# Two layers on one core: row scales of two RMS norms moved behind the matrix products

## The chip, the cores and the metric

The kernel runs on one core of a Trainium2 chip. The metric is the device time of one execution in microseconds (us), median of the runs; lower is better. TensorE (PE, with its weight loads PEld) does the matrix products, VectorE (DVE), ScalarE (ACT) and GpSimd (POOL) the element work, and SyncE (SP) issues most DMA transfers. The engines run side by side and wait for each other on semaphores.

## The reference

Two blocks on 512 rows of width 1024, all in float32, one after the other. The change lies in the first block, in two of its norms and in what comes behind them:

```python
def rmsnorm(x, g):
    y = x * lax.rsqrt(jnp.mean(jnp.square(x), axis=-1, keepdims=True) + RMS_EPS)
    return y * g

def memory_cross_attention(h, mem_n, w_q, w_kv, w_o):          # 4 heads of 256, 256 memory rows
    q = (h @ w_q).reshape(B, S, XATTN_HEADS, XATTN_HEAD_DIM)
    k, v = jnp.split(mem_n @ w_kv, 2, axis=-1)                 # reshaped to heads
    s = jnp.einsum('bshd,bmhd->bhsm', q, k) * (XATTN_HEAD_DIM ** -0.5)
    prob = jax.nn.softmax(s, axis=-1)
    return jnp.einsum('bhsm,bmhd->bshd', prob, v).reshape(B, S, D_MODEL) @ w_o

def first_block(x, mem, ...):
    h = rmsnorm(x, norm_mix)
    p = h @ w_in
    y = jnp.concatenate([retention_mixer(p[..., :RET_PROJ], ...), rwkv7_mixer(p[..., RET_PROJ:], ...)], axis=-1)
    x = x + y @ w_out
    x = x + memory_cross_attention(rmsnorm(x, norm_xattn), rmsnorm(mem, norm_mem), xattn_w_q, xattn_w_kv, xattn_w_o)
    h = rmsnorm(x, norm_mlp)
    x = x + jnp.square(jax.nn.relu(h @ mlp_w_up)) @ mlp_w_down     # width 4096
    return rmsnorm(x, norm_final)
# second_block: gated attention and a gated spatial mix, then a last norm; the change does not touch it
```

## The kernel before

Every product is done in three passes: each operand is split into a rounded high part (h) and the rest (l), and high by high, high by low and low by high are summed in PSUM (`mm3` and the loops like it). The weights come as 189 units of 128x1024, 512 KB each, streamed by SP into three `raw` buffers; `pump` makes a high part with an ACT cast and a low part with a subtraction on POOL or DVE (POOL for all units of the stretch that changes), into four pairs of buffers.

The order of the PE instructions is written out by hand. `streams` runs one main generator and a queue of side generators; at each `yield` of the main one a step passes, and a side piece spawned with a delay of so many steps is written into the PE's order when its step comes. Behind a `yield` with a name a generator goes on when that flag is set. On the other engines and in SP's queue the order comes from a scheduler that runs when the program is built, and at run time every queue goes strictly in that order.

After the mixers (`mix`) the row blocks of 128 go through `x1` and `mlp`:

- `x1` adds `y @ w_out` in two column halves j of 512 with `quad`. For j = 0 the four row blocks share each unit and finish 6 matrix multiplications apart; for j = 1 (`outer`) all four units are there and each block b finishes on its own, 24 multiplications after the one before. `quad` yields in front of every fourth multiplication.
- `add_half` adds the half to x on DVE, squares it on ACT with a sum per row, and for j = 1 multiplies x by the norm's weight row on POOL into `xg` (line 957). The weight row is a 512 KB transfer, broadcast to all partitions (`gain`).
- `norm_end` (lines 966 to 976) sums the squares, takes the root on DVE (`norm_scale`, `rsqrt`: eleven small instructions in a chain, lines 353 to 362 and 962, 963), scales `xg` by it (line 972), and 8 steps later `transp` turns the block on PE, eight 128x128 pieces into two PSUM tiles "tp" (of which there are two), each split by one ACT copy (872) and one DVE subtraction (873) of 128x512. Then the flag `norm b` is set.
- `tile_half` then multiplies the turned rows, three units for columns (rows of x) 0 to 255, then for 256 to 511: 72 multiplications of 256 columns each. Its second half waits for `norm 3`.
- The heads of the cross attention follow, with `softmax` on 128x256 tiles, then `x1`'s second pair of quads (`xattn_w_o`) with the same norm steps for `norm_mlp`, a second `tile_half` and the feed forward (`mlp`), whose sums go to x with `add_x`.

Of the kernel before, what the change touches and what calls it, by code (L numbers as in the profile page):

```python
# [82 lines left out]
def pack(inputs):  # L83

    f = {k: np.asarray(v) for k, v in inputs.items()}
# [19 lines left out]
    r, k, v = (wr[:, i * 512:(i + 1) * 512] for i in range(3))  # L105
# [71 lines left out]
    for name, key in (("w0", "rwkv_w0"), ("a0", "rwkv_a0"), ("k_k", "rwkv_k_k"), ("k_a", "rwkv_k_a"), ("r_k", "rwkv_r_k"),  # L177
# [5 lines left out]
    rows = np.concatenate([f[n].reshape(-1) for n in (  # L183
        "norm_mix", "norm_mem", "norm_xattn", "norm_mlp", "norm_final", "norm_gain_2", "final_gain_2",
        "ln_v_gain_2", "ln_v_bias_2", "q_gain_2", "k_gain_2", "b_spatial_2")])[None]
    c, cs = constants()
# [4 lines left out]
        "pos": np.ascontiguousarray(f["positions"].reshape(NB, P).T),  # L191
        "wst": np.ascontiguousarray(np.stack(units)),
        "pv": pv,
        "rows": np.ascontiguousarray(rows),
        "cst": c,
        "cs2": cs,
# [32 lines left out]
class Kern:  # L229
# [712 lines left out]
    def add_half(self, st, b, j, ps, scale=None):  # L942

        nc = self.nc
        self.add_x(b, j, ps, scale)
        x = self.x[b]
        if j == 0:
            st[b] = [self.small(3, "ss"), None]
            nc.scalar.activation(self.tmp(), x[:, 0:512], AF.Square, accum_out=st[b][0][:, 0:1])
            return  # L950
        self.flags.discard(f"norm {b}")
        ss, st[b][1] = st[b][0], self.tmp((P, 1024), "t4", 2)
        for i in range(4):
            c = slice(i * 256, i * 256 + 256)
            if i > 1:
                nc.scalar.activation(self.tmp((P, 256)), x[:, c], AF.Square, accum_out=ss[:, i - 1:i])
            nc.gpsimd.tensor_tensor(st[b][1][:, c], x[:, c], st["g"][:, c], op=ALU.mult)

    def norm_scale(self, ss, scale=1.0 / D, eps=1e-6):
        V = self.nc.vector  # L960
        v = self.small(1)
        V.tensor_reduce(v, ss, axis=AX.X, op=ALU.add)
        V.tensor_scalar(v, v, scale, eps, op0=ALU.mult, op1=ALU.add)
        return self.rsqrt(v, 1)

    def norm_end(self, st, b, dst, rs=None, wait=None):

        ss, xg = st[b]
        rs = self.norm_scale(ss) if rs is None else rs
        for h in range(2):  # L970
            c = slice(h * 512, h * 512 + 512)
            self.nc.vector.tensor_scalar(xg[:, c], xg[:, c], rs, None, op0=ALU.mult)
        yield 8
        self.transp(xg, b, dst)
        self.flags.add(f"norm {b}")

    def x1(self):
        st = {"g": self.gain("norm_xattn", 4)}
        hh, hx = self.act4((7, 8, 5, 9))

        def main():
            y1 = self.y1
            yield from self.quad(lambda k: y1[k], lambda b, ps: self.add_half(st, b, 0, ps))
            yield from self.quad(lambda k: y1[k], lambda b, ps: self.x1_post(st, b, ps, hh), outer=True)
            q = {}

            def put(t, ps):
                h = t // 2
                if t % 2 == 0:
                    q[h] = self.slab(12 + h % 2, [P, 2, 2, 512], F32R)  # L990
                self.psplit((q[h][:, 0, t % 2], q[h][:, 1, t % 2]), ps)
                if t % 2:
                    self.spawn(self.head(h, q[h]), 2)

            self.O = {}
            yield "norm 1"
            for t, ps in enumerate((yield from self.tile_half(hx, ("mm",) * 3, "norm 3"))):
                put(t, ps)
            for t in range(3, 8):
                put(t, (yield from self.tile_t(hx)))  # L1000
            st2 = self.st2 = {"g": self.gain("norm_mlp", 13)}
            self.hm, self.hmt = self.act4((2, 3, 0, 1))
            o = lambda k: self.O[k // 2][k % 2]
            yield from self.quad(o, lambda b, ps: self.add_half(st2, b, 0, ps), [f"head {h}" for h in range(4)])
            yield from self.quad(o, lambda b, ps: self.x1_post(st2, b, ps, self.hm), outer=True)

        return main()

    def rest(self):
        yield from self.x1()  # L1010
        yield from self.mlp()

    def x1_post(self, st, b, ps, dst):
        self.add_half(st, b, 1, ps)
        self.spawn(self.norm_end(st, b, dst))

    def head(self, h, q):

        pt = self.slab(4 if h % 2 == 0 else 6, [P, 2, 2, 512], F32R)

        def score(b):
            c = slice(b * 128, b * 128 + 128)
            sc = self.psum("tp", (P, 256))
            for k in range(2):
                self.mm3(sc, (q[:, 0, k, c], q[:, 1, k, c]), (self.mk[0][:, 2 * h + k], self.mk[1][:, 2 * h + k]), k == 0, k == 1)
            p = self.softmax(sc, 256, 1.0 / 16)
            yield 3
            tr = self.psum("ch", (P, 2, 128))
            for m in range(2):
                self.T.transpose(tr[:, m], p[:, m * 128:m * 128 + 128], self.ident)  # L1030
            self.psplit((pt[:, 0, :, c], pt[:, 1, :, c]), tr)

        for b in range(NB):
            self.spawn(score(b))
            yield 2
        yield 3 + 2
        o = self.slab((10, 11, 7, 8)[h], [P, 2, 2, 512], F32R)
        for d in range(2):
            ps = self.psum("ch")
            c = slice(h * 256 + d * 128, h * 256 + d * 128 + 128)  # L1040
            for m in range(2):
                self.mm3(ps, (self.mv[0][:, m, c], self.mv[1][:, m, c]), (pt[:, 0, m], pt[:, 1, m]), m == 0, m == 1)
            self.psplit((o[:, 0, d], o[:, 1, d]), ps)
            yield 1
        yield 1
        self.O[h] = [(o[:, 0, d], o[:, 1, d]) for d in range(2)]
        self.flags.add(f"head {h}")

    def softmax(self, sc, n, scale):

        nc = self.nc
        m, s = self.small(1), self.small(1)
        nc.vector.tensor_reduce(m, sc, axis=AX.X, op=ALU.max)
        nc.vector.tensor_scalar(m, m, -scale, None, op0=ALU.mult)
        p = self.tmp((P, n))
        nc.scalar.activation(p, sc, AF.Exp, bias=m, scale=scale, accum_out=s)  # L1056
        nc.vector.reciprocal(s, s)
        nc.vector.tensor_scalar(p, p, s, None, op0=ALU.mult)
        return p


    def mlp(self):
        nc = self.nc
        free = [4, 5, 6, 9, 10, 11, 7, 8]
        us = {}
        cur = {}

        def up(t, ps):
            if t % 2 == 0:
                cur["s"] = self.slab(free[(t // 2) % len(free)], [P, 2, 2, 512], F32R)  # L1070
            o = cur["s"]
            r, q = self.tmp(), self.tmp()
            nc.scalar.activation(r, ps, AF.Relu)  # L1073
            nc.gpsimd.tensor_tensor(q, r, r, op=ALU.mult)  # L1074
            self.split((o[:, t % 2, 0], o[:, t % 2, 1]), q)
            us[t] = (o[:, t % 2, 0], o[:, t % 2, 1])

        def main():
# [7 lines left out]
            for g in range(3):  # L1086
                for j in range(2):
                    for i in range(4 * j, 4 * j + 4):
                        up(8 * (g + 1) + i, (yield from self.tile_t(self.hmt)))
                    yield from self.quad(lambda k: us[8 * g + k], lambda b, ps: self.add_x(b, j, ps))  # L1090
            self.h2, self.h2t = self.act4((2, 3, 0, 1))

            def post(b, j, ps):

                self.add_x(b, j, ps)
                if j == 0:
                    self.flags.discard(f"norm {b}")
                    s0[b], s1[b] = self.small(4, "ss"), self.small(4, "ss")
                for i in (2 * j, 2 * j + 1):
                    x = self.x[b][:, i * 256:i * 256 + 256]  # L1100
                    nc.scalar.activation(self.tmp((P, 256)), x, AF.Square, accum_out=s0[b][:, i:i + 1])
                    nc.gpsimd.tensor_tensor(x, x, g1[:, i * 256:i * 256 + 256], op=ALU.mult)
                    nc.scalar.activation(self.tmp((P, 256)), x, AF.Square, accum_out=s1[b][:, i:i + 1])
                if j:
                    self.spawn(fin(b))
# [20 lines left out]
            for j in range(2):  # L1126
                yield from self.quad(lambda k: us[24 + k], lambda b, ps: post(b, j, ps), outer=True)
            yield from self.second()

        return main()  # L1130


# [570 lines left out]
```

## Time and profile before

| | us |
|---|---|
| median of 3 runs | 1331.93 |
| lowest and highest run | 1331.39, 1334.37 |
| the profiled execution, its own time | 1330.39 |
| its span, first to last instruction | 1328.6 |

All rows below come from the profiled execution. Its mean granted TensorE clock is 0.976 of full speed. The page gives busy times over the span; the chain of waits is followed back from the last instruction; the timeline lists instructions in order of time and, in square brackets, how long the engine stood idle before one and what ended that; the windows give busy time by stretch. PE is busy for 95% of the span, so what counts is where PE stands still or runs at a lower clock, and what it waits for there.

### The profile page before, as it was taken

To read this page: it belongs to the slowest core of one execution; us is meant where nothing else is said; L and a number is where in the kernel's file an instruction comes from. 1 tells how busy PE (TensorE), PEld (TensorE's weight loads), DVE (VectorE), ACT (ScalarE), POOL (GpSimd) and SP (SyncE) were. 2 spreads that over 40 slices of the span, in tenths; PEclk is the share of its full clock that TensorE was granted. 3 is DMA by queue.
4 is the path that set the end of the run, shared out by engine and by line. 5 is a ranking of instruction groups with operands and counts; after the bars stand their busy time and mean duration, and the time that the engine had idled before them with its cause. 6 is when DMAs were issued, how large, how long until landed. Compare 5 with 4: busy or idle time off the path is not lost.

```text
span 1328.6 us, 18213 instructions
## 1 busy us (share of the span) xinstructions
PE 1257.8 (95%) x6988; PEld 1043.1 (79%) x6988; DVE 699.8 (53%) x1465; ACT 507.7 (38%) x899; POOL 536.7 (40%) x544
## 2 busy tenths in 40 slices
PE   4999799998997989998999999999999999999997
PEld 4667577887895888888888888888887888788886
DVE  5667424456495275546333333332779946665355
ACT  5434323333344234433433322332534435554332
POOL 4924545135666553246311111110214563222474
PEclk9989899899999999999999999999999999999999
DMA  5223313211234422313333233333332232122321
GB/s 188 76 62 83 76 53 72 74 56 41 80 113 143 141 64 80 95 49 111 111 95 96 95 95 96 96 100 100 101 114 80 80 111 64 48 64 64 111 80 64
DMA packets 52376, 117.06 MB, mean 88 GB/s; under 512 B 23072, under 2 KB 23712, under 8 KB 52288
## 3 DMA queue, kind: packets, MB, share of 16 engines
q1 hardware_dynamic: 52112, 115.82, 28.6%
q8 instruction: 55, 0.90, 0.3%
q14 instruction: 33, 0.27, 0.1%
q0 software_dynamic: 32, 0.00, 0.0%
q10 hardware_dynamic: 144, 0.07, 0.0%
HBM read 112.46 MB, written 3.41 MB: 87 GB/s over the span
## 4 chain that ended last, share of the span: by engine, by line
PE 78%; POOL 7%; DVE 7%; issue 3%; ACT 2%; DMA 2%; SPq 0%; DVEq 0%; ACTq 0%; POOLq 0%
PE mm L220 64%; PE ch L220 7%; PE tp L220 4%; POOL s L220 3%; PE cs L220 3%; POOL o L1581 1%; DVE sm L362 1%; POOL s L1583 1%; DVE s L873 1%; DVE sm L358 1%; DMA s<-x 1%; DMA s<-dm 1%; POOL wl L220 0%; ACT t L1056 0%; ACT wh L291 0%
## 5 line engine op out<-in xcount | busy, mean ns | idle before, releaser
L220 PE MATMUL mm<-s,wh 128*128 128x512 f32 (+1 forms) x1424 | 422.5, 378 | 0.0
L220 PE MATMUL mm<-wh,s 128*128 128x512 f32 (+1 forms) x1264 | 364.1, 364 | 7.8 <-DVE s L873 7.8
L220 PEld LDWEIGHTS mm<-s,wh 128*128 128x128 f32 x1424 | 259.1, 191 | 53.2 <-issue 9.7
L220 PEld LDWEIGHTS mm<-wh,s 128*128 128x128 f32 x1264 | 231.2, 192 | 47.2 <-DVE s L873 9.6
L220 PE MATMUL mm<-s,wl 128*128 128x512 f32 (+1 forms) x704 | 263.5, 374 | 0.0
L291 ACT CAST wh<-raw 128x1024 fp32r<-128x1024 f32 x151 | 158.6, 1051 | 250.2 <-PE mm L220 220.2
L292 POOL TENSOR_TENSOR wl<-raw,wh 128x1024 fp32r<-128x1024 f32 x75 | 180.5, 2408 | 156.7 <-ACT wh L291 140.5
L220 PE MATMUL mm<-wl,s 128*128 128x512 f32 (+1 forms) x632 | 227.0, 359 | 2.0 <-POOL wl L292 1.7
L292 DVE TENSOR_TENSOR wl<-raw,wh 128x1024 fp32r<-128x1024 f32 x76 | 95.3, 1253 | 120.9 <-ACT wh L291 120.6
L220 PEld LDWEIGHTS mm<-s,wl 128*128 128x128 f32 x704 | 134.2, 191 | 21.3
L220 PEld LDWEIGHTS mm<-wl,s 128*128 128x128 f32 x632 | 121.9, 193 | 19.1 <-POOL wl L292 2.1
L1074 POOL TENSOR_TENSOR t<-t 128x512 f32<-128x512 f32 x32 | 50.0, 1563 | 214.8 <-ACT t L1073 214.8
L220 PE MATMUL mm<-s,whx 128*128 128x512 f32 (+1 forms) x336 | 100.2, 378 | 0.0
L220 PE MATMUL mm<-whx,s 128*128 128x512 f32 (+1 forms) x272 | 86.5, 377 | 0.6 <-DVE s L873 0.6
L347 DVE TENSOR_TENSOR s<-t,s 128x512 fp32r<-128x512 f32 x44 | 38.6, 877 | 69.9 <-ACT s L346 69.9
L292 POOL TENSOR_TENSOR wlx<-raw,whx 128x1024 fp32r<-128x1024 f32 x18 | 43.7, 2426 | 75.0 <-ACT whx L291 75.0
L220 PEld LDWEIGHTS mm<-s,whx 128*128 128x128 f32 x336 | 62.2, 194 | 10.6 <-DVE s L873 0.4
L220 PE MATMUL ch<-s,s 128*64 128x64 f32 (+3 forms) x504 | 65.2, 274 | 2.5 <-DVE s L873 1.8
L938 DVE TENSOR_TENSOR s<-mm,s 128x256 f32<-128x256 f32 x96 | 35.7, 419 | 58.7 <-PE mm L220 58.5
L291 ACT CAST whx<-raw 128x1024 fp32r<-128x1024 f32 x35 | 36.8, 1052 | 70.6 <-PE mm L220 54.4
L220 PE MATMUL mm<-s,wlx 128*128 128x512 f32 (+1 forms) x168 | 63.2, 376 | 0.0
L220 PEld LDWEIGHTS ch<-s,s 128*64 128x64 f32 (+2 forms) x504 | 47.0, 154 | 16.5 <-DVE s L873 3.7
(268 smaller groups left out, 1703.6 us busy)
## 6 DMA issues: line engine op xcount, KB each, us to landing
raw<-wst SPq DMA_DIRECT2D x189, 512.0 KB, 3.6
s<-x SPq DMA_DIRECT2D x8, 512.0 KB, 5.6
s<-rows SPq DMA_DIRECT2D x7, 512.0 KB, 4.0
out<-t SPq DMA_DIRECT2D x8, 256.0 KB, 2.3
t<-mem SPq DMA_DIRECT2D x2, 512.0 KB, 3.9
dm<-s SPq DMA_DIRECT2D x10, 64.0 KB, 2.0
s<-dm SPq DMA_DIRECT2D x2, 256.0 KB, 4.3
s<-dm SPq DMA_DIRECT2D x8, 64.0 KB, 2.5
```

Source lines behind the costliest of these rows:

```text
L220: r = getattr(self.eng, name)(*a, **k)
L291: (SC or nc.scalar).copy(h, r)
L292: (E or (nc.gpsimd if self.lowpart(self.nspl) else nc.vector)).tensor_tensor(l, r, h.bitcast(F32), op=ALU.subtract)
L347: self.nc.vector.tensor_tensor(dst[1], src, dst[0].bitcast(F32), op=ALU.subtract)
L358: V.scalar_tensor_tensor(t, y, h, y, op0=ALU.mult, op1=ALU.mult)
L362: V.scalar_tensor_tensor(y, t, 1.5, y, op0=ALU.add, op1=ALU.mult)
L873: (V or self.nc.vector).tensor_tensor(dst[1], ps, dst[0].bitcast(F32), op=ALU.subtract)
L938: self.nc.vector.tensor_tensor(xs, ps[:, c], xs, op=ALU.add)
L1074: nc.gpsimd.tensor_tensor(q, r, r, op=ALU.mult)
L1581: G.tensor_tensor(tv, w[:, 0:k, s:s + 1].broadcast_to([P, k, n]), m[:, s:s + 1, s + 1:32].broadcast_to([P, k, n]), op=ALU.mult)
L1583: G.tensor_tensor(w[:, 0:k, s + 1:32], w[:, 0:k, s + 1:32], tv, op=ALU.add)
```

## The change

The rows are turned without their scale, and without the weight. The weights of the two norms come as 16 columns in one small transfer (`gcol`, 64 bytes per partition) and are applied per partition in the split behind the turn: for each 128x128 piece one ACT copy with a scale and one DVE `scalar_tensor_tensor`, in place of one copy and one subtraction for four pieces. Each half is turned as soon as it is summed: half 0 of block b 3 + b steps after its sum, half 1 three steps after. One chain of roots over all four blocks (four columns) replaces the four chains. For the cross attention the scale goes into the softmax (as the scale of the exponential, and negated for the maximum); behind the squared ReLU of the feed forward the square of the scale is applied where the sums are added to x, so that 64 additions become `scalar_tensor_tensor`. The POOL multiplications by the weight rows and the two 512 KB transfers are gone.

```diff
+    def turn_half(self, st, b, j, ps, dst, delay):
+        nc = self.nc
+        self.add_x(b, j, ps)
+        if b + j == 0:
+            st["ss"] = self.small(8, "ss")
+        x = self.x[b][:, j * 512:j * 512 + 512]
+        if j:
+            self.flags.discard(f"norm {b}")
+
+        def turn():
+            h, l = dst[j]
+            c = slice(b * 128, b * 128 + 128)
+            tr = self.psum("tp", (P, 4, 128))
+            for k in range(4):
+                self.T.transpose(tr[:, k], x[:, k * 128:k * 128 + 128], self.ident)
+            for k in range(4):
+                g = st["g"][:, 4 * j + k:4 * j + k + 1]
+                nc.scalar.activation(h[:, k, c], tr[:, k], AF.Copy, scale=g)
+                nc.vector.scalar_tensor_tensor(l[:, k, c], tr[:, k], g, h[:, k, c].bitcast(F32), op0=ALU.mult, op1=ALU.subtract)
+            nc.scalar.activation(self.tmp(), x, AF.Square, accum_out=st["ss"][:, 2 * b + j:2 * b + j + 1])
+            if j == 0:
+                return
+            self.flags.add(f"norm {b}")
+            if b == NB - 1:
+                yield 5
+                v = self.small(4)
+                nc.vector.tensor_reduce(v, st["ss"].rearrange("p (b j) -> p b j", j=2), axis=AX.X, op=ALU.add)
+                nc.vector.tensor_scalar(v, v, 1.0 / D, 1e-6, op0=ALU.mult, op1=ALU.add)
+                st["scale"](self.rsqrt(v, 4))
+
+        self.spawn(turn(), delay)
+
     def x1(self):
-        st = {"g": self.gain("norm_xattn", 4)}
+        rows = self.mp.tile([P, 28], F32, name="rows")
+        g, self.sq, self.sm2 = rows[:, 0:16], rows[:, 16:24], rows[:, 24:28]
+        self.nc.sync.dma_start(g, self.A["gcol"])
+        def scale_q(rs):
+            V.tensor_scalar(self.sq[:, 0:4], rs, 1.0 / 16, None, op0=ALU.mult)
+            V.tensor_scalar(self.sq[:, 4:8], rs, -1.0 / 16, None, op0=ALU.mult)
+            self.flags.add("scale")
+        def scale_m(rs):
+            V.tensor_tensor(self.sm2, rs, rs, op=ALU.mult)
...
-            yield from self.quad(lambda k: y1[k], lambda b, ps: self.add_half(st, b, 0, ps))
-            yield from self.quad(lambda k: y1[k], lambda b, ps: self.x1_post(st, b, ps, hh), outer=True)
+            yield from self.quad(lambda k: y1[k], lambda b, ps: self.turn_half(st, b, 0, ps, hh, 3 + b))
+            yield from self.quad(lambda k: y1[k], lambda b, ps: self.turn_half(st, b, 1, ps, hh, 3), outer=True)
...
     def head(self, h, q):
+        yield "scale"
...
-            p = self.softmax(sc, 256, 1.0 / 16)
+            p = self.softmax(sc, 256, self.sq[:, b:b + 1], self.sq[:, b + 4:b + 5])
...
-                    yield from self.quad(lambda k: us[8 * g + k], lambda b, ps: self.add_x(b, j, ps))
+                    yield from self.quad(lambda k: us[8 * g + k], lambda b, ps: self.add_x(b, j, ps, self.sm2[:, b:b + 1]))
```

`norm_end` and `x1_post` are removed; the pair of quads before the feed forward changes in the same way, with the second eight weight columns and `scale_m`.

## Rows read from the trace of the kernel before

**Rows 1.** The page: busy time, share of the span, instructions of PE.
```profile
PE 1257.8 (95%) x6988; PEld 1043.1 (79%) x6988; DVE 699.8 (53%) x1465; ACT 507.7 (38%) x899; POOL 536.7 (40%) x544
```

**Rows 2.** PE timeline at both norms: start, us, engine, what, count, idle before.
```profile
476.78 0.51 PE L220 MATMUL mm<-s,whx 128*128 128x256 f32 x2
...
482.31 1.06 PE L220 MATMUL tp<-ident,t 128*128 128x128 f32 x8 [4.20 <-DVE t L972]
...
601.20 0.56 PE L220 MATMUL mm<-s,whx 128*128 128x256 f32 x2
...
606.78 1.94 PE L220 MATMUL tp<-ident,t 128*128 128x128 f32 x8 [4.20 <-DVE t L972]
```

**Rows 3.** Chain of waits in order of time, 480 to 500 us: start, us, what.
```profile
483.37 7.24 PE mm L220 x48
490.61 0.87 PE tp L220 x8
491.49 8.63 PE mm L220 x72
```

**Rows 4.** The same chain at the second norm, 600 to 616 us.
```profile
608.72 6.20 PE mm L220 x48
...
615.79 9.23 PE mm L220 x77
```

**Rows 5.** Timeline of DVE and POOL, 473 us: a root's step beside a split.
```profile
473.13 2.41 POOL L292 TENSOR_TENSOR wlx<-raw,whx 128x1024 fp32r<-128x1024 f32 x1 [0.55 <-ACT whx L291]
473.19 2.37 DVE L362 SCALAR_TENSOR_TENSOR sm<-sm,sm 128x1 f32<-128x1 f32 x1
```

**Rows 6.** Windows: stretch, length, busy of PE, PEld, DVE, ACT, POOL; clock, DMA.
```profile
482.30:486.30 4.00, 3.99 (x23) 4.00 (x24) 3.12 (x10) 2.81 (x7) 2.81 (x3) 0.63 0.52 135
...
606.70:609.20 2.50, 2.42 (x12) 2.45 (x13) 1.67 (x8) 1.75 (x5) 1.41 (x2) 0.50 0.80 198
...
340.00:350.00 10.00, 10.00 (x64) 7.36 (x64) 3.35 (x7) 2.14 (x4) 6.68 (x11) 1.00 0.30 97
```

**Rows 7.** Groups by line and form, ACT: count, busy us, mean ns, idle before.
```profile
L784 ACT ACTIVATE t<-tp,pv 128x128 f32<-128x128 f32 x16 | 6.0, 459 | 0.0
L872 ACT CAST s<-mm 128x128 fp32r<-128x128 f32 x4 | 1.1, 272 | 0.0
L949 ACT ACTIVATE t<-s 128x512 f32<-128x512 f32 x12 | 7.6, 630 | 7.0 <-DVE s L938 4.7 <-DVE s L940 2.3
```

**Rows 8.** The same for DVE.
```profile
L873 DVE TENSOR_TENSOR s<-mm,s 128x128 fp32r<-128x128 f32 x4 | 1.1, 287 | 0.5 <-ACT s L872 0.4
L938 DVE TENSOR_TENSOR s<-mm,s 128x256 f32<-128x256 f32 x96 | 35.7, 419 | 58.7 <-PE mm L220 58.5
L940 DVE SCALAR_TENSOR_TENSOR s<-mm,s 128x256 f32<-128x256 f32 x16 | 6.0, 420 | 19.0 <-PE mm L220 19.0
```

**Rows 9.** Timeline of ACT and DVE, 1013 us: two splits of one PSUM tile.
```profile
1013.35 0.58 ACT L1204 CAST s<-tp 64x512 fp32r<-64x512 f32 x1 [0.87 <-DVE s L1205]
1012.63 0.68 DVE L1205 TENSOR_TENSOR s<-tp,s 64x512 fp32r<-64x512 f32 x1
1013.97 0.69 DVE L1205 TENSOR_TENSOR s<-tp,s 64x512 fp32r<-64x512 f32 x1 [0.65 <-ACT s L1204]
```

**Rows 10.** Timeline of DVE and ACT, end of the second pair's first quad.
```profile
573.78 0.76 DVE L938 TENSOR_TENSOR s<-mm,s 128x256 f32<-128x256 f32 x2 [5.49 <-PE mm L220]
575.14 0.76 DVE L938 TENSOR_TENSOR s<-mm,s 128x256 f32<-128x256 f32 x2 [0.60 <-PE mm L220]
577.91 1.04 ACT L291 CAST wh<-raw 128x1024 fp32r<-128x1024 f32 x1
```

**Rows 11.** Waits of SP's queue for the weight rows' transfers, 325 to 400 us.
```profile
SPq L376 <- PE cs L220: 9.0, 1, 9.0
```

**Rows 12.** Timeline of SP and DVE, 405 to 415 us, end of the mixers.
```profile
405.34 0.33 SPq L281 DMA_DIRECT2D raw<-wst  x1
413.27 1.67 DVE L785 SCALAR_TENSOR_TENSOR t<-t,kt 128x512 f32<-128x512 f32 x1 [1.14 <-ACT t L784]
```

More of the change, by code (lines that the diff above doesn't have):

```diff
@@ L193, in pack @@
         "pv": pv,
+        "gcol": np.ascontiguousarray(np.concatenate([f[n].reshape(8, P).T for n in ("norm_xattn", "norm_mlp")], 1)),
         "rows": np.ascontiguousarray(rows),
@@ L950, in add_half @@
             return
-        self.flags.discard(f"norm {b}")
         ss, st[b][1] = st[b][0], self.tmp((P, 1024), "t4", 2)
@@ L964, in norm_scale @@
         return self.rsqrt(v, 1)
[L966 to L975, printed above, removed]
-    def x1(self):
-        st = {"g": self.gain("norm_xattn", 4)}
+    def x1(self):
+        rows = self.mp.tile([P, 28], F32, name="rows")
+        g, self.sq, self.sm2 = rows[:, 0:16], rows[:, 16:24], rows[:, 24:28]
+        self.nc.sync.dma_start(g, self.A["gcol"])
+        V = self.nc.vector
+        def scale_q(rs):
[4 more added lines that the diff above has]
+            V.tensor_tensor(self.sm2, rs, rs, op=ALU.mult)
+        st = {"g": g[:, 0:8], "scale": scale_q}
         hh, hx = self.act4((7, 8, 5, 9))
@@ L1000, in main @@
                 put(t, (yield from self.tile_t(hx)))
-            st2 = self.st2 = {"g": self.gain("norm_mlp", 13)}
+            st2 = {"g": g[:, 8:16], "scale": scale_m}
             self.hm, self.hmt = self.act4((2, 3, 0, 1))
             o = lambda k: self.O[k // 2][k % 2]
-            yield from self.quad(o, lambda b, ps: self.add_half(st2, b, 0, ps), [f"head {h}" for h in range(4)])
-            yield from self.quad(o, lambda b, ps: self.x1_post(st2, b, ps, self.hm), outer=True)
+            yield from self.quad(o, lambda b, ps: self.turn_half(st2, b, 0, ps, self.hm, 3 + b), [f"head {h}" for h in range(4)])
+            yield from self.quad(o, lambda b, ps: self.turn_half(st2, b, 1, ps, self.hm, 3), outer=True)
         return main()
@@ L1011, in rest @@
         yield from self.mlp()
-    def x1_post(self, st, b, ps, dst):
-        self.add_half(st, b, 1, ps)
-        self.spawn(self.norm_end(st, b, dst))
     def head(self, h, q):
+        yield "scale"
         pt = self.slab(4 if h % 2 == 0 else 6, [P, 2, 2, 512], F32R)
@@ L1047, in head, with softmax @@
         self.flags.add(f"head {h}")
-    def softmax(self, sc, n, scale):
+    def softmax(self, sc, n, scale, minus=None):
         nc = self.nc
@@ L1053, in softmax @@
         nc.vector.tensor_reduce(m, sc, axis=AX.X, op=ALU.max)
-        nc.vector.tensor_scalar(m, m, -scale, None, op0=ALU.mult)
+        nc.vector.tensor_scalar(m, m, -scale if minus is None else minus, None, op0=ALU.mult)
         p = self.tmp((P, n))
@@ L1089, in main @@
                         up(8 * (g + 1) + i, (yield from self.tile_t(self.hmt)))
-                    yield from self.quad(lambda k: us[8 * g + k], lambda b, ps: self.add_x(b, j, ps))
+                    yield from self.quad(lambda k: us[8 * g + k], lambda b, ps: self.add_x(b, j, ps, self.sm2[:, b:b + 1]))
             self.h2, self.h2t = self.act4((2, 3, 0, 1))
             def post(b, j, ps):
-                self.add_x(b, j, ps)
+                self.add_x(b, j, ps, self.sm2[:, b:b + 1])
                 if j == 0:
```

## Prediction, made before the change was run

> **What bounds the kernel now.** I read the page first: PE is busy for 95% of the span [rows 1], so time can be won only where PE stands still or runs slowly. Next comes PE's timeline with its idle times at the two norms that change. At each of them PE begins the 256-column products of `tile_half`, stops after nine, and stands for 4.20 us until DVE's line 972 has scaled a block [rows 2]. The third view says why line 972 is late: a step of the root, on one number per partition, takes 2.37 us on DVE while POOL runs a 2.41 us weight split [rows 5]; the chain of roots holds several of these, and DVE's queue behind it holds the last block's additions. The windows show what the stop leaves behind: the granted clock of the four microseconds after the first stop is 0.63 of full speed, and 0.50 in the 2.5 us after the second [rows 6]. Of the two levels that is the 1.2 GHz one for a good part of these stretches; PE had stood still before.
>
> **What the two stops cost.** From the first product of `tile_half` to the end of the second group of eight turns, the first norm takes 491.49 - 476.78 = 14.71 us and the second 615.79 - 601.20 = 14.59 us [rows 2 to 4]. In each lie 9 + 48 = 57 products and two groups of eight turns. Undisturbed, 72 such products take 8.63 us, so 0.120 each, and a group of turns 0.87 us [rows 3]. That makes 57 x 0.120 + 2 x 0.87 = 8.57 us. The stops with their slow clock cost 6.14 and 6.02 us, together 12.2 us. This is what the change can win; PE's own work (products, number of turns) stays as it is.
>
> **Part 1: turning without the scale.** The last block's turn now waits only for its addition to x. It is due three steps behind its sum, which comes out as nine 256-column products into `tile_half`: 9 x 0.120 = 1.08 us after the last sum. The addition ends about 0.03 + 0.76 = 0.8 us after it [rows 10], so PE waits 0 here, 0.3 us at most. The splits of that turn must be ready for the second half of `tile_half`, 72 products (8.6 us) after its start; they need about 1.1 + 0.4 + 3.7 = 5.2 us (part 2). `norm 1`, for the first half, is set two blocks earlier. Both stops go: -12.2 us. Next late behind them would be the weights: their splits in this stretch no longer wait behind POOL's multiplications, and one 2.4 us split [rows 5] per unit of 24 products (5.4 us) leaves room.
>
> **Part 2: the split in four pieces.** Per half block there are four ACT copies and four DVE operations of 128x128, where one of 128x512 each stood. How long is one of them? For ACT the nearest rows are 0.27 us (a plain 128x128 cast from PSUM) and 0.46 us (128x128 with two per-partition operands) [rows 7]; I take 0.40, as there is one such operand. For DVE they are 0.29 us (128x128 from PSUM) and 0.42 us (256 columns with a per-partition scale) [rows 8]; I take 0.31. Do the two engines overlap on one PSUM tile? In the second block two ACT copies and two DVE subtractions of different halves of one tile do not: the second copy stands until the first subtraction ends (1012.63 + 0.68 = 1013.31, start 1013.35), and the second subtraction starts 0.04 us after the copy [rows 9]. So four pieces alternate: 4 x (0.40 + 0.04 + 0.31 + 0.04) = 3.2 us, bounds 2.6 and 3.8. The square (0.63 us [rows 7]) overlaps only the last DVE piece, so a half block takes about 3.7 us, 3.1 to 4.3.
>
> The Trainium skill, PSUM — Partial Sum Buffer, section "PSUM bank collisions raise a hardware error", gives the reason: two engines must not touch one bank in the same quadrant of partitions in the same cycle, reads included, and the compiler's scheduler orders them. It speaks against this change, and the trace agrees (0.04 us handovers). Had the pieces overlapped, a half block would take 4 x 0.40 + 0.31 = 1.9 us and the wait below would be nil.
>
> PE feels this through the two "tp" tiles: the turn after next waits until the split has freed one. Count from the first block's sum, with 1.36 us per six products [rows 10], so 0.227 each, and 0.44 us per half turn (half of 0.87). By the order written out, turns of half 0 come behind 10, 18, 30 and 38 products, at 2.3, 4.5, 7.7 and 9.9 us; those of half 1 behind 50 and 74, at 13.1 and 19.0, and the others are wider apart. With 3.7 us the splits end at 6.4, 10.1, 13.8 and 17.5. The fourth turn waits 0.2 us for the second split, the fifth 0.5 for the third, the sixth not at all. At 3.1 us nothing waits; at 4.3 the two wait 1.4 and 1.1, 2.5 us. I take 0.7 us per norm, 1.4 in all, 0 to 5. A weight cast may stand behind the first turn's copies in ACT's queue: the fourth unit's, which starts at 577.91 when PE has freed its buffer [rows 10], 4.2 us in this count. Behind a split that ends at 6.4 it takes 1.04, and its low part 2.41 on POOL: 9.9 us, where PE needs it at about 9.7 (37 products and three half turns). So 0.2 us, 1.3 if an addition comes between; it is in the same 0 to 5.
>
> **Part 3: one chain for the roots.** Fourteen small instructions, and two for the scales, come once instead of four chains of eleven. They begin behind the last square, some 7 us after the sums, and the first exponential that needs them comes after the whole of `tile_half`, at least 17 us after. Even with three stalls of 2.4 us [rows 5] in about 3 us of work, they end 13 us after the sums. Cost nothing; if that cover were gone, PE would stand for a few us behind the first head.
>
> **Part 4: additions with a scale.** The 64 additions of the feed forward change from a plain addition to the form that the kernel's last norm already uses: 420 ns against 419 [rows 8]. Nothing.
>
> **Part 5: transfers and POOL.** Two 512 KB transfers go. Before one of them SP stood 9.0 us with the weight transfers behind it [rows 11], yet PE was busy for all of 340 to 350 us [rows 6]: no gain. The POOL multiplications are gone; POOL's work beside them was not late for PE except through DVE. The small transfer takes their place in SP's queue: nothing, if it doesn't stand there (rival 2).
>
> **Sum.** -12.2 + 1.4 = -10.8 us. The profiled execution took 1330.39 us (its span of 1328.6 and 1.8 around it) and would take 1319.6; the median of the runs is 1.54 us above that execution, so I predict 1331.93 - 10.8 = 1321.1 us.
>
> **Rivals.** (1) The alternation costs more: foreign work (casts, additions) stands in most splits, the "tp" waits come to 2.5 us per norm and the fourth unit is late by 1 us; the gain is 12.2 - 7 = 5 us: 1327. For it speaks that both engines carry casts and additions in these stretches; against it, that the turns of half 1 are 5.4 us and more apart, so that a backlog from half 0 drains.
>
> (2) Slower: the small transfer stands at the head of SP's queue. Its tile lies in memory that the mixers used. If that is a tile which the last retention block still reads (DVE's line 785, until 413.27 + 1.67 = 414.94 us [rows 12]), and it is queued ahead of the weight transfer of 405.34, that and those behind it are 9.6 us late, in a stretch where each unit feeds only 12 products (2.7 us). The gain of 10.8 us then shrinks to about 1 us: 1331. Each weight transfer further up that it is queued ahead of adds that one's distance; from 11 us of standing on the kernel is slower, and at 15 us it takes 1336. For it: the large transfers that it replaces did stand at the head of the queue [rows 11]. Against it: the tile is tiny and the first of its pool, so that it probably lies over something that was done with early.
>
> (3) The gain goes back to a resource behind the norms: the heads or the feed forward find a weight late, since PE arrives 6 us earlier. Same time, 1331. Against it: between the norms PE works without a wait, and a unit lasts 5.4 us there, over twice its split on POOL.
>
> (4) Orders shift and DVE meets fewer POOL splits at the end of the mixers, too: 3 us more gain, 1317.
>
> (5) The shared port: rows 5 show a DVE step with two inputs in SBUF standing for a POOL instruction. The pieces' DVE operations read PSUM and SBUF. If they stood as well, for 1.2 us (half a split) once in a half block, it would take 4.9 us, and the fourth and fifth turn would wait 2.6 and 1.7: 4.3 us per norm, gain 12.2 - 8.6 = 3.6 us, 1328. Against it: 96 additions of that form average 419 ns in stretches full of POOL work [rows 8]. [...]
>
> **Chances.** Forecast 0.62 (1318 to 1324), rival 1 0.14, rival 2 0.06, rival 3 0.07, rival 4 0.07, rival 5 0.04. From the median a difference below 0.2% (2.7 us) is about what a measurement of this kernel can't tell from no change. Faster takes the forecast, rivals 1, 4 and 5, less a little of rival 1: 0.85. Same: rival 3 and the mild form of rival 2, 0.08. Slower: the hard form of rival 2 and shifts of order that I can't see, 0.07. The range goes from rival 4, 1316, to 1329, past rivals 1 and 5; rivals 2 and 3 are left out.
>
> **What would show it.** In the profile after: no idle time of 4 us in PE before the turns, and a clock of 1.00 through both `tile_half` stretches; two stretches of some 8.6 + 0.4 us where 14.7 and 14.6 stood (there with two groups of turns); ACT and DVE alternating on "tp" with 0.04 us between; PE idle before half turns by some tenths, released by DVE; 420 ns for line 940 in the feed forward. The prediction is wrong if PE waits for the weight splits in the second quads, for "tp" tiles by over 2 us per norm, or if SP stands for the small transfer with weights behind it.

## The result, and the profile after

The changed kernel takes 1323.47 us, median of 8 runs (1318.68 to 1329.04), where the kernel before, run beside it, takes 1331.66 (8 runs, 1327.70 to 1334.37): a ratio of 0.9941, 95% interval 0.9917 to 0.9966. The same kernel once more, in the first experiment below, gave 0.9953 (0.9932 to 0.9974). One execution in each of norm1_only, norm2_only and norm1_64 ran at a much lower clock and is left out of their ratios; the one of norm1_64 is the profiled one (1407.51 us), so that run has no row in the table of leads. The profiled execution took 1326.15 us with a span of 1324.1, against 1330.39 and 1328.6 before. In this kernel the line numbers are higher: 221 is PE's helper, 292 and 293 are the weight casts and splits, 978 and 979 the two pieces of a turned block, 987, 988 and 354 to 363 the chain of roots.

Both stops are gone. This is PE's timeline at both norms (start, us, engine, what, count, and in brackets the idle time before it and what ended it), beside [rows 2]; the second and the fourth lines are the last half turn behind nine products of `tile_half`, where PE stood for 4.20 us before:

```profile
458.00 0.66 PE L221 MATMUL tp<-ident,s 128*128 128x128 f32 x4 [0.54 <-DVE s L979]
...
480.73 0.60 PE L221 MATMUL tp<-ident,s 128*128 128x128 f32 x4
...
577.75 0.66 PE L221 MATMUL tp<-ident,s 128*128 128x128 f32 x4 [0.48 <-DVE s L979]
...
600.42 0.60 PE L221 MATMUL tp<-ident,s 128*128 128x128 f32 x4
```

Windows from the start of each `tile_half` to 9 us behind it (length, busy time of PE, PEld, DVE, ACT, POOL, granted clock, DMA) answer [rows 6]: PE has no gap, and the clock is at its upper level throughout, where 0.63 and 0.50 stood.

```profile
479.60:488.60 9.00, 9.00 (x77) 8.96 (x75) 7.92 (x23) 3.62 (x9) 6.39 (x3) 1.00 0.67 200
599.30:608.30 9.00, 9.00 (x77) 8.97 (x76) 7.94 (x22) 3.62 (x9) 6.38 (x3) 1.00 0.67 207
```

To see where time went from there on, I set the same product beside itself in two traces: counted are only the 4936 products with a weight operand, and the start of the n-th in the changed kernel less its start in the kernel before, each from the trace's first matrix instruction (10.4 us into both timelines), is the lead. From product 1410 (437.8 us by this count in the kernel before, ahead of the first norm) to 1620 (485.1) the changed kernel gains 4.85 us, from 1860 (560.9) to 2130 (616.1) another 4.78. Then it loses: from 2130 to 3540 (935.8 us, the end of the feed forward) 2.46 us, although PE waits for nothing there. The groups by line and form between 640 and 900 us (count, busy us, mean ns) show which products do it:

```profile
L221 PE MATMUL mm<-s,wh 128*128 128x512 f32 x302 | 93.1, 390 | 0.0
L221 PE MATMUL mm<-wh,s 128*128 128x512 f32 x266 | 83.0, 390 | 0.0
...
L221 PE MATMUL mm<-whx,s 128*128 128x512 f32 x96 | 31.1, 395 | 0.0
L221 PE MATMUL mm<-s,whx 128*128 128x512 f32 x96 | 30.2, 395 | 0.0
L221 PE MATMUL mm<-s,wlx 128*128 128x512 f32 x48 | 19.0, 395 | 0.0
```

In the kernel before all eight forms of this view have a mean of 389 ns; two of them:

```profile
L220 PE MATMUL mm<-whx,s 128*128 128x512 f32 x96 | 30.5, 389 | 0.0
L220 PE MATMUL mm<-s,whx 128*128 128x512 f32 x96 | 29.6, 389 | 0.0
```

Now those whose weights lie in `whx` or `wlx`, the fourth pair of weight buffers, take 395, in either role: as the operand that streams or as the one that is loaded. These two buffers are in the SBUF pool that follows the one of the mixers (the second pool below), and the new tile `rows` (28 columns, 112 bytes in each partition, 128 with its rounding) is the first of that pool: in the program's memory plan `whx` begins at byte 202816 of a partition instead of 202688. The other buffers, `wh` and `wl`, and the tiles of the activations in the feed forward stay where they were.

### The profile page after: what moved, and what is told of

It reads as the page before. It is cut to its first block, busy times and chain, and to the rows that moved or that the text cites. A ratio compares the mean times of both kernels' runs of the same rounds, so it can differ in the third digit from the quotient of the medians.

```text
span 1324.1 us, 18154 instructions
## 1 busy us (share of the span) xinstructions
PE 1258.7 (95%) x6988; PEld 1038.4 (78%) x6988; DVE 685.5 (52%) x1440; ACT 519.5 (39%) x931; POOL 515.7 (39%) x512
## 4 chain that ended last, share of the span: by engine, by line
PE 78%; POOL 7%; DVE 6%; ACT 3%; issue 3%; DMA 2%; DVEq 0%; SPq 0%; ACTq 0%; POOLq 0%
PE mm L221 65%; PE ch L221 7%; PE tp L221 4%; PE cs L221 3%; POOL s L221 3%; POOL o L1614 1%; POOL s L1616 1%; DVE s L874 1%; DMA s<-dm 1%; ACT wh L292 1%; ACT t L1089 0%; DVE t L1091 0%; DMA s<-x 0%; POOL wl L293 0%; DVE sm L363 0%
## 5 line engine op out<-in xcount | busy, mean ns | idle before, releaser
L221 PEld LDWEIGHTS mm<-whx,s 128*128 128x128 f32 x272 | 50.1, 188 | 11.0 <-DVE s L874 1.1
```

Source lines behind the costliest of these rows:

```text
L221: r = getattr(self.eng, name)(*a, **k)
```

## The experiments

The theories: **A**, only the stops matter; **B**, the scaled additions (or the new order) slow the feed forward; **C**, formed from the first batch, the tile's place does. Beside the measured times stands the lead worked out as above; this table has it for all other runs (us, negative is a gain; norm 1 is product 1410 to 1620, norm 2 is 1860 to 2130, feed forward is 2130 to 3540).

| run | norm 1 | norm 2 | feed forward |
|---|---|---|---|
| the changed kernel | -4.85 | -4.78 | +2.46 |
| again | -4.85 | -4.83 | +2.43 |
| norm1_only | -4.85 | -0.02 | +2.55 |
| norm2_only | +0.20 | -4.84 | +2.71 |
| ff_scale | -0.06 | +1.27 | +3.04 |
| pad_only | +0.19 | +1.19 | +2.55 |
| ff_scale64 | +0.05 | +1.36 | +0.33 |
| rows64 | -4.98 | -4.88 | +0.18 |
| early_cols | -4.99 | -4.87 | +0.36 |
| norm2_64 | +0.06 | -4.88 | +0.36 |
| early_four | -5.73 | -5.62 | +0.28 |
| port_dve | -0.07 | -0.10 | +0.30 |

The +1.2 to +1.4 in three of the runs that keep the old second norm are a longer stretch of slow clock behind its stop: from 609 to 612 us the granted clock is 0.55 in pad_only, 0.90 in the kernel before. In the clock records of all three it stands at half speed for 6.8 us there, in the kernel before for 3.4.

The table ends with the feed forward. From there to the last product the six runs whose tile moves its neighbours by 128 or 32 bytes lose another 0.6 to 2.1 us, the other six between -2.3 and +0.6. Some 320 more 512-column products with `whx` or `wlx` run there, and in all six PE waits 2.4 to 2.5 us for one weight split for which it waits 1.7 in the kernel before and in the other six; why, no run separates.

### The change again, and its parts

**again** is the changed kernel as it is.

> The changed kernel once more, beside the kernel before on one chip. Theory A (the two stops of PE are gone, 6.1 and 6.0 us, less 0.5 to 1 us per norm for PSUM tiles; nothing else changed): 10 to 11 us faster than before, ratio 0.992, and in the feed forward PE's multiplications again one per 0.2267 us as in the trace of before. Rival B (the scaled additions or the new order cost the feed forward 2.4 us, which the first trace of the changed kernel shows: 333.9 us where before took 331.5): the feed forward again takes 333 to 334 us, and the gain is 7 to 8 us, ratio 0.994.

1325.07 us against 1330.43, ratio 0.9953 (0.9932 to 0.9974). The gains at the norms and the loss in the feed forward come back to within 0.1 us.

**norm1_only**: the first norm as changed, the second as before, and plain additions in the feed forward.

```diff
-            st2 = {"g": g[:, 8:16], "scale": scale_m}
+            st2 = {"g": self.gain("norm_mlp", 13)}
...
-            yield from self.quad(o, lambda b, ps: self.turn_half(st2, b, 1, ps, self.hm, 3), outer=True)
+            yield from self.quad(o, lambda b, ps: self.x1_post(st2, b, ps, self.hm), outer=True)
...
-... self.add_x(b, j, ps, self.sm2[:, b:b + 1]))
+... self.add_x(b, j, ps))
```

> Only the norm ahead of the cross attention is done in the new way; the norm ahead of the feed forward is as before, with plain additions in the feed forward. Theory A: half of the gain, 5 to 5.5 us faster than before; the stop of 4.2 us stands at the second norm alone, with its slow clock behind it. Rival B: also about 5 us, as the scaled additions are not in it; then the full change gives less than twice this.

1327.95 us, ratio 0.9983 (0.9960 to 1.0007). The trace has the full gain at the first norm, and the loss in the feed forward with plain additions: B's scaled additions are not its cause.

**norm2_only**: the reverse, with the scaled additions.

```diff
-        st = {"g": g[:, 0:8], "scale": scale_q}
+        st = {"g": self.gain("norm_xattn", 4)}
...
-            yield from self.quad(lambda k: y1[k], lambda b, ps: self.turn_half(st, b, 1, ps, hh, 3), outer=True)
+            yield from self.quad(lambda k: y1[k], lambda b, ps: self.x1_post(st, b, ps, hh), outer=True)
```

> Only the norm ahead of the feed forward is done in the new way, with scaled additions in the feed forward; the norm ahead of the cross attention is as before. Theory A: 5 to 5.5 us faster than before, and this and the run with the first norm alone add up to the full change. Rival B: the feed forward loses 2.4 us, so about 3 us faster.

1329.71 us, ratio 0.9993 (0.9971 to 1.0014): again the gain at its norm, and the loss behind it.

**ff_scale**: the kernel before, with only the additions scaled, by a column of ones in a new tile of 4 columns.

```diff
+        self.ones = self.mp.tile([P, 4], F32, name="ones")
+        self.nc.gpsimd.memset(self.ones, 1.0)
...
-... self.add_x(b, j, ps))
+... self.add_x(b, j, ps, self.ones[:, b:b + 1]))
```

> The kernel before with one edit: the 64 additions of the feed forward are multiplications by a per-partition column of ones with an addition, in the form of the changed kernel. Theory A: no difference (within 1 us), the additions take 420 ns as before, the feed forward 331.5 us. Rival B: 2 to 3 us slower than before, with PE's multiplications in the feed forward spaced by more than 0.2267 us.

1336.02 us, ratio 1.0048 (1.0030 to 1.0067): slower by 5.6 us of the medians. By itself this run speaks for B, norm1_only against it. What all four runs with a loss share is a new small tile at the head of the second pool. That made theory C.

### The place of the tile

**pad_only**: the kernel before with such a tile, filled once, and nothing else.

```diff
+        pad = self.mp.tile([P, 28], F32, name="pad")
+        self.nc.gpsimd.memset(pad, 0.0)
```

> The kernel before with one more tile of 28 columns at the head of the second pool, set to zero once and never read: nothing is computed differently, but the four-buffer weight tiles of that pool (whx, wlx) and the slabs behind it begin 128 bytes later in each partition. Theory C (place of the tile): products with whx or wlx take 0.232 to 0.234 us instead of 0.227, the other 512-column products stay at 0.227, and the kernel is 4 to 6.5 us slower than before (ratio 1.003 to 1.005). Theories A (only the two stops matter) and B (the scaled additions slow the feed forward): same as before within 0.1%, all products at 0.227 us.

1336.41 us against 1331.59, ratio 1.0040 (1.0017 to 1.0063). A tile that nobody reads makes the kernel 4.8 us slower. Its groups by line and form, 640 to 900 us, show the same split as the changed kernel:

```profile
L220 PE MATMUL mm<-s,wh 128*128 128x512 f32 x329 | 101.4, 389 | 0.0
L220 PE MATMUL mm<-wh,s 128*128 128x512 f32 x240 | 74.8, 389 | 0.0
...
L220 PE MATMUL mm<-whx,s 128*128 128x512 f32 x95 | 30.7, 395 | 0.0
L220 PE MATMUL mm<-s,whx 128*128 128x512 f32 x96 | 30.1, 395 | 0.0
```

and PE's timeline (start first) shows the pace: three products take 0.70 us (700.43 to 701.13, 701.13 to 701.83), 0.233 each.

```profile
700.43 0.63 PE L220 MATMUL mm<-s,whx 128*128 128x512 f32 x2
700.89 0.40 PE L220 MATMUL mm<-s,wlx 128*128 128x512 f32 x1
701.13 0.62 PE L220 MATMUL mm<-s,whx 128*128 128x512 f32 x2
701.60 0.39 PE L220 MATMUL mm<-s,wlx 128*128 128x512 f32 x1
701.83 0.62 PE L220 MATMUL mm<-s,whx 128*128 128x512 f32 x2
```

**rows64**: the changed kernel with its tile widened, so that what lies behind it moves by 256 bytes instead of 128.

```diff
-        rows = self.mp.tile([P, 28], F32, name="rows")
+        rows = self.mp.tile([P, 64], F32, name="rows")
```

> The changed kernel with its tile of columns widened from 28 to 64 columns (256 bytes in each partition instead of 128), the other columns unused. Theory C: the products with whx and wlx are back at 0.227 us, the feed forward's stretch is back at 331.5 us, and the time is 10 to 12 us below before (ratio 0.991 to 0.9925), so 4 to 6 us below the changed kernel. Theory B: feed forward still 333.9 us, time as the changed kernel (ratio 0.994 to 0.996). A: as the changed kernel too.

1321.20 us, ratio 0.9926 (0.9902 to 0.9951): 10.4 us below before. One number in the kernel gives back what C said. Three products take 0.68 us (724.54 to 725.22), 0.227 each, and the groups are even again:

```profile
724.54 0.61 PE L221 MATMUL mm<-s,whx 128*128 128x512 f32 x2
724.99 0.39 PE L221 MATMUL mm<-s,wlx 128*128 128x512 f32 x1
725.22 0.61 PE L221 MATMUL mm<-s,whx 128*128 128x512 f32 x2
```

```profile
L221 PE MATMUL mm<-s,wh 128*128 128x512 f32 x288 | 88.6, 389 | 0.0
...
L221 PE MATMUL mm<-whx,s 128*128 128x512 f32 x100 | 31.9, 389 | 0.0
L221 PE MATMUL mm<-s,whx 128*128 128x512 f32 x89 | 27.5, 389 | 0.0
```

**ff_scale64**: ff_scale with its tile of ones 64 columns wide.

```diff
-        self.ones = self.mp.tile([P, 4], F32, name="ones")
+        self.ones = self.mp.tile([P, 64], F32, name="ones")
```

> The kernel before with the 64 additions of the feed forward scaled by a column of ones that stands in a tile of 64 columns (256 bytes), where the run with 4 columns stood 32 bytes off. Theory C: products at 0.227 us, time same as before within 0.15% (the scaled additions cost nothing). Theory B: 5 to 7 us slower than before, as with the 4-column tile (ratio 1.004 to 1.006).

1331.24 us, ratio 0.9998 (0.9972 to 1.0025). The scaled additions cost no time that can be measured; B has fallen.

**early_cols**: the changed kernel with its 28 columns in the constant pool, which lies ahead of all others, loaded at the start by ACT's queue.

```diff
+        self.gcol = self.cp.tile([P, 28], F32, name="rows")
+        nc.scalar.dma_start(self.gcol[:, 0:16], A["gcol"])
...
-        rows = self.mp.tile([P, 28], F32, name="rows")
+        rows = self.gcol
...
-        self.nc.sync.dma_start(g, self.A["gcol"])
```

> The changed kernel with its tile of 28 columns in the first, constant pool instead, loaded once at the start by ACT's queue: every later tile of every pool is 128 bytes later, so the tiles that a product reads stand to each other as in the kernel before, but 128 bytes from where they stood; SP no longer waits for the columns in the norm. If only the distance between the two operands counts (C, relative): products at 0.227 us, time 10 to 12.5 us below before (ratio 0.9905 to 0.9925). If the place itself counts (C, absolute): all 512-column products at 0.232 us or more, some 15 us slower than the changed kernel (ratio over 1.004). Theory B: as the changed kernel less at most 1 us.

1319.54 us, ratio 0.9916 (0.9882 to 0.9949). Here every buffer that these products read is 128 bytes from its old place, `whx` at 202816 as in the slow kernel, yet the products keep the pace of before (feed forward +0.36 us): what counts is how the operands lie to each other, not where they lie. SP's wait for the small transfer (below) is gone too, but what that is worth can't be told from rows64 by these intervals.

### The norms, with the place mended

**norm1_64** and **norm2_64** are norm1_only and norm2_only with the tile of 64 columns.

```diff
-        rows = self.mp.tile([P, 28], F32, name="rows")
+        rows = self.mp.tile([P, 64], F32, name="rows")
```

> The first norm of the changed kernel with the second norm and the plain additions of the kernel before, and the tile of columns 64 wide (256 bytes), so that no product's operands move against each other. If the two norms bring their gains separately and the place of the tiles was all that hid them (theory C): 4.5 to 6 us below before (ratio 0.9955 to 0.9966), where the same kernel with 28 columns stood at 0.9983. If the first norm's gain went elsewhere (the resource behind it): 0.9983 again.

> The second norm of the changed kernel and its scaled additions with the first norm of the kernel before, the tile of columns 64 wide. Theory C: 4.5 to 6 us below before (ratio 0.9955 to 0.9966), and with the run of the first norm alone the two gains add up to that of the whole change with 64 columns (10 to 12 us); with 28 columns this kernel stood at 0.9993. If the scaled additions or the code behind eat it: 0.998 or more.

1325.29 us, ratio 0.9961 (0.9936 to 0.9986), and 1325.50 us, ratio 0.9975 (0.9952 to 0.9997), against 1330.01. The first is what was expected; the second's ratio is weaker than expected, while its trace has the same 4.88 us at its norm. Together 6.4 per mille, 8.5 us, where rows64 has 7.4 per mille; the intervals allow that they add up.

**early_four**: early_cols with the turns in two kinds of PSUM tiles by turns.

```diff
-            tr = self.psum("tp", (P, 4, 128))
+            tr = self.psum(("tp", "ch")[b % 2], (P, 4, 128))
```

> The changed kernel with its columns loaded early into the constant pool (as in the run early_cols) and the turns of the norm in two kinds of PSUM tiles by turns (tp for blocks 0 and 2, ch for 1 and 3), so that a turn never asks for a tile whose pieces are still being read. If the 0.5 us for which PE waits for such a tile at each norm is time on the path: 1.0 us below early_cols (ratio to before 0.9905 to 0.992), no wait of PE for a tp tile at the norms. If something else ends last: the same as early_cols.

1317.08 us, ratio 0.9927 (0.9899 to 0.9954): the times can't tell it from early_cols (1319.54, 0.9916), and the ratio misses the expected 0.9905 to 0.992; the trace can. The half turn that waited 0.52 us there comes without a wait,

```profile
458.22 0.60 PE L221 MATMUL tp<-ident,s 128*128 128x128 f32 x4
```

and the norms gain 5.73 and 5.62 us instead of 4.99 and 4.87: a wait for a "tp" tile costs 0.74 and 0.75 us a norm. Its median is the lowest of all, its ratio is not.

**port_dve**: the kernel before with the eight weight splits around its two norms on DVE instead of POOL.

```diff
-        self.lowpart = lambda u: u <= 3 or 31 <= u < 79 or 145 <= u
+        self.lowpart = lambda u: u <= 3 or 31 <= u < 55 or 59 <= u < 71 or 75 <= u < 79 or 145 <= u
```

> The kernel before with the weight splits of the eight units around the two norms on DVE instead of POOL, so that nothing on POOL holds the port when DVE computes the last root of a norm; eight splits of 1.25 us each are added to DVE. If it was POOL's splits (2.3 us each) that stretched the last root's steps to 1.80 and 2.26 us and so made PE's two stops of 4.2 us (port theory): the stops shrink to 1 to 2.5 us each, the time falls by 3 to 7 us (ratio 0.995 to 0.998). If the stop is the chain of one block's turn itself (steps of 0.17 us, the scaling, the turn), or DVE's own splits take the place of POOL's: stops of 4 us or more, time as before or up to 2 us slower.

1332.72 us, ratio 1.0031 (1.0009 to 1.0052): not faster, some 3 to 4 us slower, and both stops are as long as they were. PE's and DVE's timelines at the first norm:

```profile
483.91 1.12 PE L220 MATMUL tp<-ident,t 128*128 128x128 f32 x8 [4.21 <-DVE t L972]
```

```profile
477.74 0.20 DVE L358 SCALAR_TENSOR_TENSOR sm<-sm,sm 128x1 f32<-128x1 f32 x1
477.87 1.21 DVE L292 TENSOR_TENSOR wl<-raw,wh 128x1024 fp32r<-128x1024 f32 x1
479.00 0.15 DVE L362 SCALAR_TENSOR_TENSOR sm<-sm,sm 128x1 f32<-128x1 f32 x1
479.07 1.21 DVE L292 TENSOR_TENSOR wl<-raw,wh 128x1024 fp32r<-128x1024 f32 x1
480.21 0.74 DVE L938 TENSOR_TENSOR s<-mm,s 128x256 f32<-128x256 f32 x2
480.87 0.56 DVE L358 SCALAR_TENSOR_TENSOR sm<-sm,sm 128x1 f32<-128x1 f32 x1
481.36 1.21 DVE L292 TENSOR_TENSOR wl<-raw,wh 128x1024 fp32r<-128x1024 f32 x1
482.50 0.67 DVE L362 SCALAR_TENSOR_TENSOR sm<-sm,sm 128x1 f32<-128x1 f32 x1
```

Without POOL's splits no root step stretches to 2.3 us as in [rows 5] (at most 0.78 around both norms), but three splits of 1.21 us now stand among the steps in DVE's own queue. The rival came true. So the run doesn't show what the stops would be with a free DVE and no split beside it on POOL; it shows that the chain on PE's path waits for whatever else DVE has to do. That the change works by taking the chain off that path fits it, and the changed kernel's trace, in which the same chain is still long and PE has no stop. Where the slower time went stays open: in the profile the last product comes only 0.05 us later than in the kernel before, both counted from the first matrix instruction.

## Why the prediction came out as it did

The forecast was 1321.1 us, faster; measured were 1323.47 us, faster. The mechanism held, and one term was missing from the sum. Norms and feed forward of the table add up to -7.2 us, of the -8.2 measured.

**The stops.** Predicted -12.2 us with -10.8 left after the waits for "tp" tiles; the trace has -4.85 - 4.78 = -9.6 us, and with the operands in place -9.9 (rows64). Without those waits (early_four) it is -11.35, so the 12.2 were over-sized by 0.8 us, 0.4 a norm; where these went no run separates.

**The alternation.** Put at 0.7 us a norm between bounds of 0 and 2.5; 0.74 and 0.75 were measured by the difference of early_four and early_cols, of which 0.52 us each are PE's idle time in early_cols (0.54 and 0.48 in the changed kernel). One piece was to take 0.40 on ACT, 0.31 on DVE and two handovers of 0.04, 0.79 us in all. The timelines of ACT and DVE show 0.79 from one copy to the next (459.48 to 460.27), as 0.37 and 0.35 with 0.03 and 0.04 between; that the sum is met to 0.01 is luck, as one size was put too high by 0.03 and the other too low by 0.04:

```profile
459.48 0.37 ACT L978 ACTIVATE s<-tp,rows 128x128 fp32r<-128x128 f32 x1 [0.42 <-DVE s L979]
460.27 0.37 ACT L978 ACTIVATE s<-tp,rows 128x128 fp32r<-128x128 f32 x1 [0.42 <-DVE s L979]
```

```profile
459.88 0.35 DVE L979 SCALAR_TENSOR_TENSOR s<-tp,rows,s 128x128 fp32r<-128x128 f32 x1 [0.44 <-ACT s L978]
460.67 0.35 DVE L979 SCALAR_TENSOR_TENSOR s<-tp,rows,s 128x128 fp32r<-128x128 f32 x1 [0.44 <-ACT s L978]
```

That the wait comes to the predicted size is luck as well. I had the fourth half turn wait 0.2 us and the fifth 0.5, for splits of 3.7 us each; they wait for nothing. It is the third turn that waits, at 458.00, for the first split, which takes 5.4 us, from 452.55 to 457.94 (the first of the two pieces in the last line below). Between its pieces stand additions, squares, a weight cast and pieces of the second split, as rival 1 had it:

```profile
452.55 0.35 ACT L978 ACTIVATE s<-tp,rows 128x128 fp32r<-128x128 f32 x1
454.61 1.03 ACT L292 CAST wh<-raw 128x1024 fp32r<-128x1024 f32 x1
457.59 0.61 DVE L979 SCALAR_TENSOR_TENSOR s<-tp,rows,s 128x128 fp32r<-128x128 f32 x2 [0.18 <-ACT s L978]
```

Rival 1's price of some 3.5 us a norm did not come, as the turns behind it wait for nothing.

**The chain of roots.** Here a step failed, without a price. I let the chain run behind the last splits and gave those 5.2 us from the start of `tile_half`. But the last square stands ahead of the last split's pieces in ACT's queue (480.69), the chain begins behind it at 481.45, and in DVE's queue its steps stand among those pieces; two of them last until one of POOL's splits of 2.4 us ends. DVE's timeline at the first norm:

```profile
481.64 1.97 DVE L988 TENSOR_SCALAR sm<-sm 128x4 f32<-128x4 f32 x1
...
484.12 2.12 DVE L355 TENSOR_SCALAR sm<-sm 128x4 int32<-128x4 int32 x1
...
488.32 0.35 DVE L979 SCALAR_TENSOR_TENSOR s<-tp,rows,s 128x128 fp32r<-128x128 f32 x1
```

So the last piece ends at 488.67, 9.0 us after the start of `tile_half` at 479.64. PE goes on to the second half's products at 488.72, without a wait:

```profile
488.60 0.28 PE L221 MATMUL mm<-s,wl 128*128 128x256 f32 x1
488.72 0.39 PE L221 MATMUL mm<-s,whx 128*128 128x256 f32 x2
```

The cover of 3.4 us that I counted on was thus more than used up, 9.0 us against 8.6. PE has no wait because there was more cover than I counted, which is luck: `tile_half` takes the eight column pieces in order, three products each, and the last split makes only the last four. So the first twelve products of the second half read what was turned earlier; the first that reads a piece of this split starts at 490.14, the first that reads the low part of the last piece at 491.32, 2.65 us after it was done.

**The scaled additions.** Predicted 420 ns, "nothing"; they take 478 ns (group of the changed kernel):

```profile
L941 DVE SCALAR_TENSOR_TENSOR s<-mm,rows,s 128x256 f32<-128x256 f32 x64 | 27.6, 478 | 18.3 <-PE mm L221 18.2
```

The row that I took them from [rows 8] has no tile as its scale. On DVE that is 64 x 0.058 = 3.7 us, and none of it can be seen in the time (ff_scale64: 0.9998, and +0.33 us in the feed forward).

**The small transfer.** Rival 2's mechanism was there, in a mild form. The waits of SP's queue have it standing for line 786, which is line 785 of the kernel before [rows 12], as that rival said, but for 3.0 us and not 9.6:

```profile
SPq L1003 <- DVE t L786: 3.0, 1, 3.0
```

SP's timeline shows why: it was queued behind the weight transfer of 411.93, and the next ones follow right behind it.

```profile
411.93 0.33 SPq L282 DMA_DIRECT2D raw<-wst  x1
415.32 0.33 SPq L1003 DMA_DIRECT2D rows<-gcol  x1
415.74 2.55 SPq L282 DMA_DIRECT2D raw<-wst  x2
```

By the prediction's last sentence this was a sign of being wrong: SP stands for the small transfer with weights behind it. It cost nothing that the trace shows: PE has no wait for weights behind it in either norm.

**The missing term.** I priced each instruction that the change adds, and none of the bytes. The tile of columns has a place of its own and moves its neighbours: +2.5 us in the feed forward, and on the whole 4.8 us in a kernel in which nothing else changes (pad_only; 2.3 to 8.4 by its interval), 2.2 to 5.0 us between the two results of the changed kernel (-8.2 and -5.4) and rows64 (-10.4), though again and rows64 ran on different chips. With the place mended the measured -10.4 and -12.1 us (early_cols) stand on both sides of the -10.8 of the sum. Rival 3, a loss behind the norms, named the sign, but looked for a late weight; from the second norm to the end of the feed forward PE waits for none, the products themselves are slower. Only in the second block one such wait grows by 0.7 us.

## What to carry to other kernels

When a change adds a tile, even one that nobody reads in the hot loop, look at which buffers move and compare the mean time of one product by its operands before and after; a difference of 6 ns between forms that were equal is the sign, and where a pace has slipped without a wait, padding the tile (here to 256 bytes) costs nothing to try. A chain of many tiny steps should lie where its length doesn't matter: here it took as long as what stood between its steps in DVE's queue and the splits that ran beside it on POOL. Where a theory explains the first runs, test it with a kernel that does only the suspected thing (here an unread tile) before the edit is blamed for what its memory does.

## What the runs showed of the hardware

**Products and the distance of their operands.** In the feed forward, 512-column products whose streaming operand and loaded operand have starts that differ by a multiple of 256 bytes within the partition keep 0.2267 us from start to start (before, rows64, ff_scale64, and early_cols, where all starts are 128 bytes further). Where one of the two is 128 bytes off (the changed kernel, pad_only) or 32 bytes (ff_scale), the products that read it take 0.232 to 0.234 us. A product's own two operands are not the whole condition: near the end of pad_only, 16 products stream `whx` against a tile of the same pool, so that both have moved by the 128 bytes, and still take 0.230 to 0.238 us (0.227 in the kernel before, 0.226 in rows64); the products beside them have theirs off. Products of 256 columns with `whx` or `wlx` show no loss: a median of 0.119 to 0.120 us in pad_only, 0.120 before. Other distances were not tried, and what in the chip causes it stays open. The Trainium skill, SBUF — State Buffer, section "Who interferes with whom", gives TensorE two read ports that are independent, one for the streaming operand and one for the weight load, and says that only the port pair of DVE and GpSimd contends. By that the distance of two operands would not be expected to matter; the measurement differs, by 6 ns in 227, and decides.

**A slow clock behind the two stops.** In both `tile_half` stretches the granted clock fell to 0.63 and 0.50 of full speed behind the stops [rows 6] and stays at 1.00 without them. Of the 5.73 and 5.62 us that the norms give back in early_four, 4.20 each are idle time; an estimate of the slow clock from [rows 6], 4.00 x 0.37 = 1.5 and 2.50 x 0.50 = 1.25 us, covers most of the other 1.5 and 1.4.

**Small DVE steps and POOL's splits.** TENSOR_SCALAR steps on 4 columns, with a single operand and in SBUF, stood for 1.97 and 2.12 us beside weight splits of 2.4 us on POOL, as the one-column steps with two did before [rows 5]. The pieces on DVE, which read one operand from PSUM and one from SBUF, average 348 ns over 64 of them and did not stand: rival 5 did not come.
